# RWKV chunks of a hybrid trunk: one elementwise instruction for both directions or both heads, score products in column halves of the array

## The chip, the cores and the metric

One core of a Trainium2 chip runs the whole program in one launch. The metric is the device time of one execution in microseconds: the kernel before takes 3569.35 us, the median of 3 runs (3568.7 to 3575.61). The engines named here are TensorE (PE in the profile, PEld for its weight loads), VectorE (DVE), ScalarE (ACT), GpSimd (POOL) and SyncE (SP), whose in-order queue issues most DMAs.

## What is computed

A trunk of two layers over 1024 latent and 256 context tokens. Each layer has a token mixer with three groups of heads (RWKV-7 in both directions, windowed attention, neighbourhood attention) and a mixture of experts. The change touches the RWKV group alone: four heads of 64 channels, a state of 64 by 64 per head and direction, fed token by token.

```python
def _rwkv7_step(state, inp):
    r, w, k, v, kk, a = inp
    sk = jnp.einsum('dbhvk,dbhk->dbhv', state, kk)
    state = state * w[..., None, :] - sk[..., :, None] * (kk * a)[..., None, :] + v[..., :, None] * k[..., None, :]
    return state, jnp.einsum('dbhvk,dbhk->dbhv', state, r)
```

Here `d` is the direction (2), `h` the head (4). The 1280 tokens are taken in the order context, latents for the forward direction and with both parts reversed for the backward one; the two outputs of a token are added later.

## The kernel before

The recurrence runs in chunks of 64 tokens. `rwkv()` makes 10 steps per layer; a step handles 128 tokens, that is two chunks (index `c`), of both directions (`d`). Heads lie in pairs: `hp` is the pair (2), and `e` the head in it, whose 64 channels stand in partitions 0 to 63 or 64 to 127 (`hom[e]`, the home half). So a step has 16 units of (d, hp, c, e), in 8 columns of two halves.

`front(st)` prepares a step, one step ahead of its use: `ld` and `lwa` are loaded, the matmuls of L733 give decay and gate inputs, four scans (L744) accumulate the log decay, and the products `L1` (kk and r times decays, L774 and L775: head 0 on VectorE, head 1 on GpSimd), `bk` (L782 on VectorE, L783 on GpSimd) and `bw` (L786) follow.

The step itself then does this, all in fp32:

- L807: 16 transposes turn `bw` into two PSUM tiles `pb`, one for each head, which ScalarE copies to `L2` (L810).
- L822: 16 matmuls `pa`, with 64 rows and all 128 columns of the array, multiply the pair (b, k) of a unit with its pair (kk, r). One matmul so gives four 64 by 64 blocks. VectorE takes them out under masks: `L1`'s other half (L827), `Ly` (L829), and `low` of the backward direction (L831).
- L838: 8 matmuls `pf` give the forward direction's `low`, masked by L839.
- `inv16()` inverts the 16 by 16 diagonal blocks of `low`: `low` goes to DRAM (`lan`) and comes back with another layout (`al`), VectorE does some 30 small instructions (L948 to L955), and the result goes by DRAM (`inv`) into `z16` and `zt16`.
- `mm8` (L851) is called three times with 16 matmuls each, `pe`, `pzt` and `pz`, 64 columns wide, and VectorE combines them (L855 to L857): this joins the blocks of 16 to blocks of 32. L862 to L876 join those to 64.
- Two substeps `s` then advance the state `X`: `px` (L902), a copy `xy` on ScalarE, `pu` (L910), its negation into `X` (L911, L912), `pmy` (L924, L922), the next state (L928), and the output `ys`, four adds of 64 by 128 (L933). `xw` (L895) is the decayed state on GpSimd; `new_pvu` (L711) copies the values into the next `X` with four ScalarE instructions.
- At the step's end two DMAs store `ys` (L938); `values()` loads the next values with two DMAs.

Beside this chain TensorE has independent work: the projections for the two attentions (`in_BC`: L526 to L528 and L537 to L539, products of fp16 high and low parts) are generated piecewise by `more()` between the parts of a step. Every engine runs its own list in order. The lists are written at build time by a scheduler, which mixes the chain of one step, the preparation of the next and the projections.

## Time and profile before

| | before |
|---|---|
| median of 3 runs | 3569.35 us (3568.7 to 3575.61) |
| the profiled execution's own time | 3569.75 us |
| its span in the profile | 3568.1 us |
| TensorE busy over the span | 2943.9 us |
| VectorE busy over the span | 2283.7 us |
| ScalarE busy over the span | 1544.1 us |
| GpSimd busy over the span | 996.8 us |
| mean granted TensorE clock | 0.889 |

The span runs from the first to the last instruction of one execution; 1.65 us of the execution's time lie around it. The RWKV recurrence with the projections beside it takes the stretch from 225 to 734 us in the first layer and from 2004 to 2490 us in the second. Elsewhere (the input projection, attention, output projection, experts) nothing is changed. Busy time of TensorE counts a matmul from its start to its modelled end, so that many overlap; how fast a group of equal matmuls really goes is read from the distance of the starts of groups that follow each other. An fp32 matmul is two records in the trace (a transpose one), so that x32 stands for 16 matmuls. Tiles `L1`, `z16_0` and the like are named `L`, `z` in the rows, and the three uses of `mm8` all stand at L851.

### The profile page before, as it was taken

The page shows a single profiled execution, that of the slowest core. Times are in us where ns is not written, and L with a number is a line of the kernel's source. Part 1 is how long each engine was busy: PE and PEld are TensorE (multiplying, and loading weights), DVE is VectorE, ACT ScalarE, POOL GpSimd, SP SyncE. Part 2 cuts the span into 40 slices and gives each one's busy share as a digit, 9 for nine tenths or more (in the row PEclk, how much of TensorE's full clock was granted, in tenths as well). Part 3 has the DMA queues.
Part 4 walks back from the last instruction along what each step waited for, and adds up shares of the span by engine and source line. Part 5 has one row for each costly group of instructions (what it writes and reads, how often), then busy time and mean ns, then how long its engine had stood idle before and what let it go on. Part 6 is the DMA issues. An engine that isn't in the chain of part 4 may idle for free. (4 is left out here: it accounts for less than half of the span.)

```text
span 3568.1 us, 71262 instructions
## 1 busy us (share of the span) xinstructions
PE 2943.9 (83%) x28620; PEld 1838.5 (52%) x28620; DVE 2283.7 (64%) x4614; ACT 1544.1 (43%) x2769; POOL 996.8 (28%) x998
## 2 busy tenths in 40 slices
PE   7998888989997888888737988898889867777875
PEld 4656556666754434444326555666666443334432
DVE  4257777467768474547688677783776845555765
ACT  4334344346633153546544434343465314434641
POOL 2022443134424111110065225331433321101103
PEclk9989899989998889899868988899899978889977
DMA  9864343372455889999862432443732769999976
GB/s 372 282 206 110 79 108 87 92 212 78 114 202 170 291 327 353 365 378 355 343 228 80 156 100 71 105 104 87 204 107 72 257 238 352 379 389 379 340 265 226
DMA packets 469245, 773.13 MB, mean 217 GB/s; under 512 B 211920, under 2 KB 341616, under 8 KB 452272
## 3 DMA queue, kind: packets, MB, share of 16 engines
q1 hardware_dynamic: 431824, 697.84, 56.9%
q0 software_dynamic: 36368, 68.07, 5.7%
q8 instruction: 228, 3.74, 0.4%
q10 hardware_dynamic: 720, 2.62, 0.3%
q14 instruction: 105, 0.86, 0.1%
HBM read 653.31 MB, written 114.97 MB: 215 GB/s over the span
## 5 line engine op out<-in xcount | busy, mean ns | idle before, releaser
L1662 PE MATMUL pgate<-wgp,hT 128*64 128x512 f16 (+2 forms) x1704 | 371.7, 388 | 130.8 <-ACT wgp L1611 76.6
L1662 PEld LDWEIGHTS <-hT 128*64 128x64 f16 (+2 forms) x3408 | 210.9, 110 | 365.9 <-issue 195.5
L526 PE MATMUL acc<-hH,wH 128*128 128x256 f16 (+2 forms) x1040 | 344.8, 335 | 15.2 <-DVE hH L483 13.0
L527 PE MATMUL acc<-hL,wH 128*128 128x256 f16 (+2 forms) x1040 | 345.3, 333 | 9.5 <-POOL hL L484 9.4
L528 PE MATMUL acc<-hH,wL 128*128 128x256 f16 (+2 forms) x1040 | 345.3, 333 | 0.0
L1662 PE MATMUL pgate<-wup,hT 128*32 128x256 f16 (+1 forms) x1224 | 212.8, 362 | 24.5 <-DVE wup L1612 13.7
L1193 POOL TENSOR_SCALAR s<-s,rd 128x640 f32<-128x640 f32 (+2 forms) x216 | 172.8, 800 | 211.5 <-DVE rd L1189 96.4
L1702 PE MATMUL pd<-wdp,gT 128*64 128x512 f16 (+2 forms) x1704 | 213.1, 358 | 21.7 <-DVE gT L1689 14.9
L1612 DVE SCALAR_TENSOR_TENSOR wgp<-wg,wgp 128x2048 f16<-128x2048 f32 x74 | 166.6, 2286 | 93.4 <-ACT wgp L1611 93.4
L1620 POOL DMA_INDIRECT xg<-hmoe,map x69 | 78.3, 1136 | 527.7 <-PE ptx L1626 491.8
L1612 DVE SCALAR_TENSOR_TENSOR wdp<-wd,wdp 128x2048 f16<-128x2048 f32 x74 | 166.6, 2288 | 71.8 <-ACT wdp L1611 71.8
L1182 ACT ACTIVATE s<-s,nm 128x640 f32<-128x640 f32 (+2 forms) x216 | 164.5, 763 | 68.2 <-DVE nm L1179 50.4
L1206 PE MATMUL po<-pt,vt 128*64 128x128 f32 x1920 | 170.5, 291 | 19.6 <-DVE pt L1197 15.0
L1612 DVE SCALAR_TENSOR_TENSOR wup<-wu,wup 128x2048 f16<-128x2048 f32 x74 | 166.2, 2287 | 31.1 <-ACT wup L1611 31.0
L1291 PE MATMUL acco<-wo,o 128*128 128x512 f16 x756 | 175.9, 386 | 0.0
L1611 ACT ACTIVATE wgp<-wg 128x2048 f16<-128x2048 f32 x74 | 137.6, 1903 | 74.1 <-DMA wg<-w_gate 56.7
L1611 ACT ACTIVATE wdp<-wd 128x2048 f16<-128x2048 f32 x74 | 137.2, 1902 | 73.7 <-DMA wd<-w_down 69.3
L1702 PEld LDWEIGHTS <-gT 128*64 128x64 f16 (+2 forms) x1704 | 95.1, 105 | 124.9 <-DVE gT L1689 20.7
L1715 POOL DMA_DIRECT2D ys<-y x66 | 51.8, 784 | 384.4 <-DVE y L1709 215.5
L1611 ACT ACTIVATE wup<-wu 128x2048 f16<-128x2048 f32 x74 | 137.3, 1904 | 44.4 <-DMA wu<-w_up 41.7
L1163 PE MATMUL pss<-k,qs 128*128 128x256 f16 (+1 forms) x552 | 129.3, 272 | 31.8 <-DVE mx L1176 18.3
L1670 ACT ACTIVATE sg<-pgate 64x256 f32<-64x256 f32 (+2 forms) x86 | 42.7, 496 | 246.9 <-PE pgate L1662 246.8
(420 smaller groups left out, 7429.1 us busy)
## 6 DMA issues: line engine op xcount, KB each, us to landing
wu<-w_up SPq DMA_DIRECT2D x64, 2048.0 KB
wd<-w_down SPq DMA_DIRECT2D x64, 2048.0 KB
wg<-w_gate SPq DMA_DIRECT2D x64, 2048.0 KB
wmod<-w_mod SPq DMA_DIRECT2D x96, 512.0 KB
w<-w_in SPq DMA_DIRECT2D x41, 512.0 KB
ld<-ys SPq DMA_DIRECT2D x40, 384.0 KB
z<-inv SPq DMA_DIRECT2D x80, 128.0 KB
ys<-y POOLq DMA_DIRECT2D x20, 512.0 KB, 10.5
```

Source lines behind the costliest of these rows:

```text
L526: self.nc.tensor.matmul(ov, H[:, k, :], hh, start=k == 0, stop=False)
L527: self.nc.tensor.matmul(ov, H[:, k, :], hl, start=False, stop=False)
L528: self.nc.tensor.matmul(ov, Lo[:, k, :], hh, start=False, stop=k == KD - 1)
L1163: te.matmul(pss[:, o:o + n], qs[:, e, Q], k1[:, e, k0:k0 + n], start=True, stop=False)
L1182: a.activation(s2[:, e, :nk], s2[:, e, :nk], AF.Exp, bias=nm[:, e:e + 1], scale=1.0 / SS, accum_out=den[:, e:e + 1])
L1193: g.tensor_scalar(s2[:, e, :nk], s2[:, e, :nk], rd[:, e:e + 1], SC_Q, OP.mult, OP.mult)
L1206: te.matmul(po[64 * e:64 * e + 64, 0:P], vt[:, kb, 64 * e:64 * e + 64], pt[:, e, x * P:x * P + P], start=x == 0, stop=x == len(kbs) - 1)
L1291: te.matmul(acc, o[:, zo, k] if k < KD - 1 else self.og_last[:, zo, tok], wo[:, zw, k, c], start=k == 0 and y == 0, stop=k == KD - 1 and y ...
L1611: nc.scalar.mul(t[:, 0, c], w[:, c], SC_W)
L1612: nc.vector.scalar_tensor_tensor(t[:, 1, c], w[:, c], SC_W, t[:, 0, c], OP.mult, OP.subtract)
L1662: te.matmul(p[off + i * m:off + i * m + m, :n], part(hT, zh)[:, k, o:o + m], part(w, zw)[:, k, i * n:i * n + n], start=k == 0 and y == 0, ...
L1702: te.matmul(t, part(gT, zh)[:, k, :m], part(wd, zw)[:, k, i * n:i * n + n], start=k == 0 and y == 0, stop=k == 3 and y == len(parts) - 1)
```

## The change

The layout of the tiles is turned so that equal operations of both directions, or of both heads of a pair, are one instruction, and the score products are regrouped by what is taken from them:

- `bw`'s transposes: for head 0 as before; for head 1 each one becomes two ordinary fp32 matmuls with the identity, which put the two 64 by 64 blocks into the halves that the later steps want.
- `pa` gives way to `pk` (k against kk and r, 128 columns, written to the other half of the partitions: 64 rows and 64 columns of the array, both heads in one PSUM tile), `pr` (b against r) and `pf` (b against kk), 16 matmuls each.
- The masks: `L1` as before (4 instructions of 64 by 512), `Ly` one of 128 by 512 for four of 64 by 256, `low` one of 128 by 512 for three.
- `L1`'s products are all on VectorE, 4 of 64 by 512 instead of 4 of 64 by 256 there and 4 on GpSimd. `bk`: one of 128 by 512 on each of VectorE and GpSimd, for two of 64 by 512. The scans: two of 256 for four of 128.
- `mm8` computes and combines only the halves of the columns that can change: 32 columns for 64, and VectorE's three instructions have 256 elements for 512.
- `ys`: one add of 128 by 256 per substep for four of 64 by 128, stored at once by two DMAs per substep (four per step for two). The values come by three DMAs per step for two, and `new_pvu` makes two copies of 64 by 512 for four of 64 by 256. `L2`'s copies are two of 128 by 512 for four of 128 by 256.

```diff
+        E4 = rp.tile([P, 8, 64], F32, name=f"E4{l}")
+        g.memset(E4, 0.0)
...
         vt = {}
         def values(st):
             vt[st] = rp.tile([P, 2, 2, 2, 64], F32, tag="vt", name="vt", bufs=2)
-            for d, seg in enumerate((FSEG[st], BSEG[st])):
-                nc.sync.dma_start(vt[st][:, d], self.vst[:, 2 * seg:2 * seg + 2])
+            nc.sync.dma_start(vt[st][:, :, 0], self.vst[:, 2 * FSEG[st]:2 * FSEG[st] + 2])
+            for s in range(2):
+                nc.sync.dma_start(vt[st][:, s, 1], self.vst[:, 2 * BSEG[st] + 1 - s])
         def new_pvu(st, s):
             t = rp.tile([P, 2, 2, 2, 2, 64], F32, tag="pvu", name="pvu", bufs=2)
-            for d in range(2):
-                for e in range(2):
-                    o = hom[1 - e]
-                    a.copy(t[o, d, :, :, e, :], vt[st][o, d, s if d == 0 else 1 - s].unsqueeze(1).to_broadcast([64, 2, 2, 64]))
+            for e in range(2):
+                o = hom[1 - e]
+                a.copy(t[o, :, :, :, e, :].rearrange("p x d h v -> p x (d h) v"),
+                       vt[st][o, s].rearrange("p d h v -> p (d h) v").unsqueeze(1).to_broadcast([64, 2, 4, 64]))
             return t
...
             for d in range(2):
-                for hp in range(2):
-                    v.tensor_tensor_scan(cum[:, d, hp], k2("scan"), th[:, d, hp], 0.0, OP.mult, OP.add)
+                v.tensor_tensor_scan(cum[:, d].rearrange("p h t -> p (h t)"), k2("scan"), th[:, d].rearrange("p h t -> p (h t)"), 0.0, OP.mult, OP.add)
...
-            L1v = L1.rearrange("p d c h e s t -> p d h e s c t")
-            bku = bk.rearrange("p d h c s t -> p (d h c) s t")
-            for d in range(2):
-                for e in range(2):
-                    eng = v if e == 0 else g
-                    eng.tensor_tensor(L1v[hom[e], d, :, e, e], chv(kk_)[hom[e], d], chv(ex)[hom[e], d], OP.mult)
-                    eng.tensor_tensor(L1v[hom[e], d, :, e, 1 - e], chv(r_)[hom[e], d], chv(cum)[hom[e], d], OP.mult)
+            def pieces(x):
+                return x.rearrange("p d h (c t) -> p d h c t", t=64).rearrange("p d h c t -> p d (h c) t")
             def units(x):
                 return x.rearrange("p d h (c t) -> p (d h c) t", t=64)
+            bku = bk.rearrange("p d h c s t -> p (d h c) s t")
+            v.scalar_tensor_tensor(bku[:, :, 0], units(b2), 0.5, units(wv), OP.mult, OP.mult)
+            g.tensor_tensor(bku[:, :, 1], units(kd), units(wv), OP.mult)
+            L1p = L1.rearrange("p d h c e s t -> p d (h c) e s t")
             for e in range(2):
                 o = hom[e]
-                v.scalar_tensor_tensor(bku[o, :, e], units(b2)[o], 0.5, units(wv)[o], OP.mult, OP.mult)
-                g.tensor_tensor(bku[o, :, 1 - e], units(kd)[o], units(wv)[o], OP.mult)
+                for i, (x, y) in enumerate(((kk_, ex), (r_, cum))):
+                    v.tensor_tensor(L1p[o, :, :, e, i], pieces(x)[o], pieces(y)[o], OP.mult)
...
-                        for e in range(2):
-                            te.transpose(pbs[e][:, i * 64:i * 64 + 64], bw[hom[e], d, hp, c].rearrange("p s t -> p (s t)"), self.ident[hom[e], hom[e]])
+                        o = slice(i * 64, i * 64 + 64)
+                        te.transpose(pbs[0][:, o], bw[hom[0], d, hp, c].rearrange("p s t -> p (s t)"), self.ident[hom[0], hom[0]])
+                        for z in range(2):
+                            te.matmul(pbs[1][hom[1 - z], o], bw[hom[1], d, hp, c, z, :], self.ident[hom[1], hom[1]], start=True, stop=True)
             for e, pb in enumerate(pbs):
-                for d in range(2):
-                    a.copy(L2[:, d, :, :, e].rearrange("p c h t -> p h c t"), pb[:, 256 * d:256 * d + 256].rearrange("p (h c t) -> p h c t", h=2, c=2))
...
+                a.copy(L2[:, :, :, :, e].rearrange("p d h c t -> p (d h c) t"), pb.rearrange("p (u t) -> p u t", t=64))
...
             for d in range(2):
-                pas = [ps.tile([P, 512], F32, tag=tag, name="pa") for _ in range(2)]
+                pk = ps.tile([P, 4, 128], F32, tag=tag, name="pk")
                 for hp in range(2):
                     for c in range(2):
-                        i = 2 * hp + c
                         for e in range(2):
-                            te.matmul(pas[e][:, i * 128:i * 128 + 128], bk[hom[e], d, hp, c].rearrange("p s t -> p (s t)"),
-                                      L1[hom[e], d, c, hp, e].rearrange("p s t -> p (s t)"), start=True, stop=True)
-                for e, pa in enumerate(pas):
-                    home, oth = hom[e], hom[1 - e]
-                    pav = pa.rearrange("p (h c s t) -> p h c s t", h=2, c=2, s=2)
-                    v.tensor_tensor(L1[oth, d, :, :, e].rearrange("p c h s t -> p h c (s t)"), pav[oth].rearrange("p h c s t -> p h c (s t)"),
-                                    mask(f"mL1_{d}", oth, 128), OP.mult)
-                    v.tensor_tensor(Ly[home, d].rearrange("p c h t -> p h c t"), pav[home, :, :, 1 - e], mask(f"mR_{d}", home, 64), OP.mult)
-                    if d == 1:
-                        v.tensor_tensor(low[home, 1], pav[home, :, :, e], mask("mLow", home, 64), OP.mult)
-            pf = ps.tile([P, 512], F32, tag=tag, name="pf")
-            for hp in range(2):
-                for c in range(2):
-                    for e in range(2):
-                        i = 2 * hp + c
-                        te.matmul(pf[hom[e], i * 64:i * 64 + 64], L1[hom[e], 0, c, hp, e, e, :], bk[hom[e], 0, hp, c, e, :], start=True, stop=True)
-            v.tensor_tensor(low[:, 0], pf[:, 0:256].rearrange("p (h c t) -> p h c t", h=2, c=2), mask("mLow", slice(0, 128), 64), OP.mult)
+                            te.matmul(pk[hom[1 - e], 2 * hp + c], bk[hom[e], d, hp, c, 1, :],
+                                      L1[hom[e], d, hp, c, e].rearrange("p s t -> p (s t)"), start=True, stop=True)
+                for e in range(2):
+                    o = hom[1 - e]
+                    v.tensor_tensor(L1[o, d, :, :, e].rearrange("p h c s t -> p (h c) (s t)"), pk[o],
+                                    k2(f"mL1_{d}")[o].unsqueeze(1).to_broadcast([64, 4, 128]), OP.mult)
+            pr = ps.tile([P, 8, 64], F32, tag=tag, name="pr")
+            pf = ps.tile([P, 8, 64], F32, tag=tag, name="pf")
+            for d in range(2):
+                for hp in range(2):
+                    for c in range(2):
+                        for e in range(2):
+                            i = 4 * d + 2 * hp + c
+                            b_, K_, r1 = bk[hom[e], d, hp, c, 0, :], L1[hom[e], d, hp, c, e, 0, :], L1[hom[e], d, hp, c, e, 1, :]
+                            te.matmul(pr[hom[e], i], b_, r1, start=True, stop=True)
+                            x, y = (K_, b_) if d == 0 else (b_, K_)
+                            te.matmul(pf[hom[e], i], x, y, start=True, stop=True)
+            v.tensor_tensor(Ly.rearrange("p d h c t -> p d (h c) t"), pr.rearrange("p (d u) t -> p d u t", d=2),
+                            k2("mR").rearrange("p (d t) -> p d t", d=2).unsqueeze(2).to_broadcast([P, 2, 4, 64]), OP.mult)
+            v.tensor_tensor(low.rearrange("p d h c t -> p (d h c) t"), pf, k2("mLow").unsqueeze(1).to_broadcast([P, 8, 64]), OP.mult)
...
             def mm8(name, lt, rh):
-                o = psi.tile([P, 512], F32, tag="i", name=name)
+                o = psi.tile([P, 8, 2, 16], F32, tag="i", name=name)
                 for u in range(8):
                     for e in range(2):
-                        te.matmul(o[hom[e], u * 64:u * 64 + 64], lt[hom[e], u, :], rh[hom[e], u, :], start=True, stop=True)
-                return o.rearrange("p (u t) -> p u t", t=64)
-            E = rp.tile([P, 8, 64], F32, tag="E", name="E", bufs=1)
-            v.tensor_tensor(E, mm8("pe4", lowu, zt16), k2("mE4").unsqueeze(1).to_broadcast([P, 8, 64]), OP.mult)
-            v.tensor_tensor(zt16, zt16, mm8("pzt", z16, E), OP.subtract)
-            v.tensor_tensor(z16, z16, mm8("pz", E, z16), OP.subtract)
+                        te.matmul(o[hom[e], u], lt[hom[e], u, :], rh[hom[e], u], start=True, stop=True)
+                return o
+            lo16, up16 = halves(z16)[:, :, :, 0], halves(zt16)[:, :, :, 1]
+            Eh = halves(E4)[:, :, :, 1]
+            v.tensor_tensor(Eh, mm8("pe4", lowu, up16), k2("mE4").rearrange("p (g t) -> p g t", t=16).unsqueeze(1).to_broadcast([P, 8, 2, 16]), OP.mult)
+            pzt = mm8("pzt", z16, Eh)
+            v.tensor_tensor(up16, up16, pzt, OP.subtract)
+            v.tensor_tensor(lo16, lo16, mm8("pz", E4, lo16), OP.subtract)
...
-            ys = rp.tile([P, 2, 2, 2, 64], F32, tag="ys", name="ys")
...
+                cs = (s, 1 - s)
...
-                for d in range(2):
-                    c = s if d == 0 else 1 - s
-                    for hp in range(2):
-                        for e in range(2):
-                            for sl in range(2):
-                                te.matmul(px[hom[sl], d, hp, e, :], L1[:, d, c, hp, e, sl, :], X[:, d, 0, hp, e, :], start=True, stop=True)
+                for sl in range(2):
+                    for d in range(2):
+                        for hp in range(2):
+                            for e in range(2):
+                                te.matmul(px[hom[e ^ sl], sl, d, hp, :], L1[:, d, hp, cs[d], e, sl, :], X[:, 0, d, hp, e, :], start=True, stop=True)
...
-                for e in range(2):
-                    o = hom[1 - e]
-                    for d in range(2):
-                        c = s if d == 0 else 1 - s
-                        v.tensor_tensor(ys[o, d, c], pm[o, 1, d], xy[o, d, :, e, :], OP.add)
+                        v.tensor_tensor(nx[hom[e], 0, :, :, e, :], pm[hom[e], 0], xw[hom[e]], OP.add)
+                ys = rp.tile([P, 2, 2, 64], F32, tag="ys", name="ys", bufs=2)
+                v.tensor_tensor(ys, pm[:, 1], xy[:, 1], OP.add)
+                for d in range(2):
+                    nc.sync.dma_start(y_d[d, 2 * seg[d] + cs[d]], ys[:, d])
...
-            for d in range(2):
-                nc.sync.dma_start(y_d[d, 2 * seg[d]:2 * seg[d] + 2].rearrange("c p h t -> p c h t"), ys[:, d])
```

The scheduler writes new lists for all engines. Three places, all in the first layer's step 4 (counted from 0), show what the prediction speaks of.

TensorE, the transposition of `bw`; `pu` belongs to the state's chain of an earlier step, `prope` and `acc` are projections. Before:

```order
L528 MATMUL acc<-hH_223,wL 128x512
L807 MATMUL pb<-c_58,bw 128x64 x3
L910 MATMUL pu_4020<-xy,z_1_3895 64x64 x4
L910 MATMUL pu_4020<-xy,z_0_3891 64x64 x4
L807 MATMUL pb<-c_58,bw 128x64 x13
L1066 MATMUL prope<-qf,c_58 128x512
```

and in the change:

```order
L812 MATMUL pb<-c_58,bw 64x64 x2
L932 MATMUL pmy<-pvu,L_3756 64x64
L810 MATMUL pb<-c_58,bw 128x64
L932 MATMUL pmy<-pvu,L_3756 64x64 x7
L930 MATMUL pmy<-pvu,Ly 64x64 x8
L812 MATMUL pb<-c_58,bw 64x64 x2
L810 MATMUL pb<-c_58,bw 128x64
```

Sixteen transposes in two runs became eight single transposes, each followed by two 64 by 64 matmuls, with the state's `pmy` among them.

TensorE, the score products (`px` and `pe` belong to the chains of earlier steps). Before, with eight more `pa` somewhat earlier:

```order
L902 MATMUL px<-pvu,L_3062 64x64 x16
L851 MATMUL pe_4409<-z_1_4405,low 64x64
L822 MATMUL pa<-L_4215,bk 128x128 x3
L851 MATMUL pe_4409<-z_1_4405,low 64x64 x15
L822 MATMUL pa<-L_4215,bk 128x128 x5
L528 LDWEIGHTS wL
```

and in the change:

```order
L822 MATMUL pk<-L_4233,bk 64x128 x6
L859 MATMUL pe_4444<-z_1_4441,low 64x32
L822 MATMUL pk<-L_4233,bk 64x128 x7
L859 MATMUL pe_4444<-z_1_4441,low 64x32 x15
L822 MATMUL pk<-L_4233,bk 64x128 x3
```

The `pa` of the two heads stand in separate runs, since each head has its own PSUM tile; the 16 `pk` of both heads stand closer, head after head. A piece of projection later the change has this, where before 8 `pf` stood:

```order
L836 MATMUL pr<-L_4233,bk 64x64 x6
L859 MATMUL pzt<-E_1987,z_0_4437 64x32 x16
L839 MATMUL pf<-bk,L_4233 64x64 x6
L836 MATMUL pr<-L_4233,bk 64x64
L839 MATMUL pf<-bk,L_4233 64x64
```

There are 32 of these in all, and from the last rows on `pr` and `pf` take turns.

VectorE, the masks of the score products and the work of the next step between them. Before:

```order
L855 TENSOR_TENSOR E<-pe_4409,c_1967 128x512
L775 TENSOR_TENSOR L_4725<-ld,cum 64x2x2x64 x2
L827 TENSOR_TENSOR L_4215<-pa,c_1967 64x2x2x128
L829 TENSOR_TENSOR Ly<-pa,c_1967 64x2x2x64
L831 TENSOR_TENSOR low<-pa,c_1967 64x256
```

and in the change:

```order
L826 TENSOR_TENSOR L_4233<-pk,c_1967 64x4x128 x2
L864 TENSOR_TENSOR E_1987<-pe_4444,c_1967 128x16x16
L826 TENSOR_TENSOR L_4233<-pk,c_1967 64x4x128 x2
L504 SCALAR_TENSOR_TENSOR wL<-w,wH 128x1024
L866 TENSOR_TENSOR z_1_4441<-z_1_4441,pzt 128x16x16
L867 TENSOR_TENSOR z_0_4437<-z_0_4437,pz 128x16x16
L840 TENSOR_TENSOR Ly<-pr,c_1967 128x512
L842 TENSOR_TENSOR low<-pf,c_1967 128x512
```

Before, the last three rows come once more for the other head, and two pairs of L827 and L829 stand earlier. In the change `Ly` and `low` are one row each, after the combination to blocks of 32 of the step before.

## Rows read from the trace of the kernel before

**Rows 1.** The page's first part: busy us, share and instructions of each engine

```profile
PE 2943.9 (83%) x28620; PEld 1838.5 (52%) x28620; DVE 2283.7 (64%) x4614; ACT 1544.1 (43%) x2769; POOL 996.8 (28%) x998
```

**Rows 2.** Windows of the mixing stretches: length, PE, PEld, DVE, ACT, POOL busy, PEclk

```profile
225.00:734.00 509.00, 447.83 (x6042) 321.00 (x6039) 336.26 (x779) 199.66 (x496) 179.05 (x177) 0.91 0.40 107
2004.00:2490.00 486.00, 432.47 (x5742) 305.93 (x5738) 333.82 (x759) 190.21 (x477) 176.43 (x163) 0.89 0.36 96
```

**Rows 3.** TensorE's waits, first layer (two), then second; total us, times, longest

```profile
PE pe L851 <- DMA z<-inv: 27.2, 12, 4.2
...
PE pmy L924 <- DVE pvu L912: 6.1, 5, 2.7
...
PE pmy L924 <- DVE pvu L912: 19.3, 5, 9.2
```

**Rows 4.** Windows of L822, L851, L807, L838 alone, in that order: sum rows

```profile
sum 995.00, PE 82.27 PEld 67.84; mean PE 41.13 PEld 33.92
...
sum 995.00, PE 86.23 PEld 73.14; mean PE 43.12 PEld 36.57
...
sum 995.00, PE 19.35 PEld 14.76; mean PE 9.67 PEld 7.38
...
sum 995.00, PE 15.13 PEld 12.07; mean PE 7.56 PEld 6.04
```

**Rows 5.** TensorE's timeline: start us, us, line, names, shapes, count

```profile
306.74 1.15 PE L851 MATMUL pzt<-E,z 64*64 64x64 f32 x32
307.82 1.16 PE L822 MATMUL pa<-L,bk 64*128 64x128 f32 x16
308.91 0.23 PE L538 MATMUL accn<-wH,hL 128*128 128x128 f16 x1
```

**Rows 6.** The same view, a few us later

```profile
312.68 1.16 PE L822 MATMUL pa<-L,bk 64*128 64x128 f32 x8
313.76 0.69 PE L862 MATMUL pe<-z,low 32*32 32x32 f32 x32
314.38 0.68 PE L838 MATMUL pf<-bk,L 64*64 64x64 f32 x16
```

**Rows 7.** The same view, where two shapes of the array alternate

```profile
299.81 0.33 PE L851 MATMUL pe<-z,low 64*64 64x64 f32 x2 [3.35 <-DMA z<-inv]
300.07 0.34 PE L807 MATMUL pb<-c,bw 64*128 64x64 f32 x4
300.34 0.23 PE L537 MATMUL accn<-wH,hH 128*128 128x128 f16 x1
```

**Rows 8.** VectorE's groups by line, 225 to 690 us (busy us, mean ns)

```profile
L827 DVE TENSOR_TENSOR L<-pa,c 64x512 f32<-64x512 f32 x40 | 27.4, 684 | 16.6 <-PE pa L822 16.3
L775 DVE TENSOR_TENSOR L<-ld,cum 64x256 f32<-64x256 f32 x20 | 24.4, 1257 | 0.1
L782 DVE SCALAR_TENSOR_TENSOR bk<-th,wv 64x512 f32<-64x512 f32 x20 | 21.6, 1080 | 0.6
L774 DVE TENSOR_TENSOR L<-ld,ex 64x256 f32<-64x256 f32 x20 | 19.3, 997 | 0.5 <-ACT ex L755 0.4
L933 DVE TENSOR_TENSOR ys<-pmy,xy 64x128 f32<-64x128 f32 x76 | 18.5, 283 | 0.3
L829 DVE TENSOR_TENSOR Ly<-pa,c 64x256 f32<-64x256 f32 x40 | 16.9, 422 | 0.6
```

**Rows 9.** GpSimd's group of the same kind, same stretch

```profile
L774 POOL TENSOR_TENSOR L<-ld,ex 64x256 f32<-64x256 f32 x20 | 19.1, 974 | 50.9 <-ACT ex L755 47.5 <-DMA z<-inv 3.4
```

**Rows 10.** VectorE's timeline inside one inversion

```profile
333.07 1.82 DVE L782 SCALAR_TENSOR_TENSOR bk<-th,wv 64x512 f32<-64x512 f32 x2
...
337.25 2.92 DVE L775 TENSOR_TENSOR L<-ld,cum 64x256 f32<-64x256 f32 x2
340.10 1.26 DVE L954 TENSOR_TENSOR zl<-zl,il 64x44 f32<-64x44 f32 x1
```

**Rows 11.** Waits of SyncE's DMA queue, first layer

```profile
SPq L938 <- DVE ys L933: 16.1, 3, 12.7
```

More of the change, by code (lines that the diff above doesn't have):

```diff
@@ L190, in _consts @@
     for k in range(2):
-        d[f"mL1_{k}"] = np.concatenate([np.concatenate([im[k], sm[k]], 1), np.concatenate([sm[k], im[k]], 1)], 0)
-        d[f"mR_{k}"] = np.concatenate([im[k], im[k]], 0)
+        d[f"mL1_{k}"] = np.tile(np.concatenate([sm[k], im[k]], 1), (2, 1))
+    d["mR"] = np.tile(np.concatenate(im, 1), (2, 1))
     d["mLow"] = np.concatenate([lo, lo], 0)
@@ L195, in _consts @@
     e4 = ((q[:, None] // 32 == q[None, :] // 32) & (q[:, None] % 32 < 16) & (q[None, :] % 32 >= 16)).astype(np.float32)
-    d["mE4"] = np.concatenate([e4, e4], 0)
-    d["scan"] = np.tile((np.arange(128) % 64 != 0).astype(np.float32), (128, 1))
+    d["mE4"] = np.tile(e4[:, q % 32 >= 16], (2, 1))
+    d["scan"] = np.tile((np.arange(256) % 64 != 0).astype(np.float32), (128, 1))
     d["i16"] = np.tile(np.eye(16).reshape(1, 256), (128, 1))
@@ L882, in rwkv @@
                 for e in range(2):
[L883 removed]
+                    g.memset(X[hom[e], 0, :, :, e, :], 0.0)
             if st < 9:
                 values(st + 1)
[L887 removed]
             for s in range(2):
                 last = st == 9 and s == 1
+                cs = (s, 1 - s)
                 if not last:
@@ L906, in rwkv @@
                 for d in range(2):
-                    c = s if d == 0 else 1 - s
                     for hp in range(2):
                         for e in range(2):
-                            te.matmul(pu2[hom[e], d, hp, :], tt[d][hom[e], hp, c, :], xy[hom[e], d, hp, e, :], start=True, stop=True)
-                a.mul(X[0:64, :, 1, :, 0, :], pu2[0:64], -1.0)
-                v.tensor_scalar_mul(X[64:128, :, 1, :, 1, :], pu2[64:128], -1.0)
+                            te.matmul(pu2[hom[e], d, hp, :], tt[d][hom[e], hp, cs[d], :], xy[hom[e], 0, d, hp, :], start=True, stop=True)
+                a.mul(X[0:64, 1, :, :, 0, :], pu2[0:64], -1.0)
+                v.tensor_scalar_mul(X[64:128, 1, :, :, 1, :], pu2[64:128], -1.0)
                 pm = psc.tile([P, 2, 2, 2, 64], F32, tag=tagc, name="pmy")
@@ L916, in rwkv @@
                     for d in range(2):
-                        c = s if d == 0 else 1 - s
                         for hp in range(2):
                             for e in range(2):
-                                U = X[:, d, 1, hp, e, :]
+                                U = X[:, 1, d, hp, e, :]
                                 if y:
-                                    te.matmul(pm[hom[1 - e], 1, d, hp, :], Ly[hom[e], d, c, hp, :], U[hom[e]], start=True, stop=True)
+                                    te.matmul(pm[hom[1 - e], 1, d, hp, :], Ly[hom[e], d, hp, cs[d], :], U[hom[e]], start=True, stop=True)
                                 else:
-                                    te.matmul(pm[hom[e], 0, d, hp, :], L2[:, d, c, hp, e, :], U, start=True, stop=True)
+                                    te.matmul(pm[hom[e], 0, d, hp, :], L2[:, d, hp, cs[d], e, :], U, start=True, stop=True)
                 if not last:
@@ L927, in rwkv @@
                     for e in range(2):
-                        v.tensor_tensor(nx[hom[e], :, 0, :, e, :], pm[hom[e], 0], xw[hom[e]], OP.add)
-                for e in range(2):
-                    o = hom[1 - e]
-                    for d in range(2):
-                        c = s if d == 0 else 1 - s
-                        v.tensor_tensor(ys[o, d, c], pm[o, 1, d], xy[o, d, :, e, :], OP.add)
+                        v.tensor_tensor(nx[hom[e], 0, :, :, e, :], pm[hom[e], 0], xw[hom[e]], OP.add)
[3 more added lines that the diff above has]
+                    nc.sync.dma_start(y_d[d, 2 * seg[d] + cs[d]], ys[:, d])
                 if not last:
```

7 lines of the change are left out of this document (3 added, 4 removed).

## The prediction

> **What bounds the kernel now.** The page's first part comes first: over the whole span TensorE is the busiest engine, with 83%, and VectorE follows with 64% [rows 1]. Such shares mix stages, so the next view is the windows of the two stretches that the change touches [rows 2]. There the reader should see that TensorE is busy for 447.83 of 509 us and for 432.47 of 486, so it idles for 61.2 + 53.5 = 114.7 us. VectorE is busy for some 334 us in each, about two thirds. Nothing else is near. The reason lies in the order of the lists: TensorE has the projections to fill its gaps, so that what a chain of waits costs appears only where the list has put an instruction too early. TensorE's work therefore sets the length, plus what it idles.
>
> The waits say what it idles for [rows 3]. In the first layer `mm8`'s first use waits 27.2 us, in 12 waits, for the `z` that the inversion sends back by DMA; and the state's `pmy` waits for VectorE's negation (L912) 6.1 us there and 19.3 us in the second layer. So the waits lead to VectorE's queue, directly or through the inversion, which is VectorE's work too. The timeline of VectorE inside one inversion shows why it is late [rows 10]: the next step's products stand between its small instructions, L782's pair takes 1.82 us, L775's 2.92, and one small instruction of 44 elements takes 1.26, while `ys` adds of 128 elements take 0.283 on average [rows 8]. GpSimd does its share of the same products then, at 0.974 us for 256 elements [rows 9], while VectorE's L829 does as many in 0.422. The two engines slow each other down.
>
> So there are two accounts: what TensorE must do, which the change alters in four places, and what it idles, which the change shortens through VectorE.
>
> **TensorE's account**, in busy time of both layers. The lines concerned take 82.3 us (`pa`), 86.2 (`mm8`), 19.4 (`pb`) and 15.1 (`pf`) [rows 4]. Prices at full clock come from the distance of starts; the granted clock is 0.91 and 0.89 [rows 2], so I divide new work by 0.9.
>
> *`pb`.* Eight transposes a step are now each followed by two 64 by 64 matmuls: 160 turns in all. Where the trace changes shape in this way [rows 7], one lone 64\*64 matmul costs 0.26 us up to the next group (299.81 to 300.07), and four 64\*128 transposes 0.27 (300.07 to 300.34). A turn then costs at least 0.26 and a quarter of 0.27, 0.33 us, and at most 0.53; I take the middle, 0.43: 160 x 0.43 / 0.9 = 76 us, which is 57 more than now. No row shows a 64\*128 and a 64\*64 group in different row halves of the array one by one; if such run side by side, nothing is added. Ends: 0 and (0.53) 75. I take 57 because rows 7 are nearest. The Trainium skill, TensorEngine Tiling (Array Packing), Key Properties, says that changing the tiling mode, not just the tile, drains the engine; by that the turns cost the 57 us, without it nothing, and the trace agrees with the rule in rows 7.
>
> *`pk`.* Eight `pa` of both heads taken in turn need 1.09 us (307.82 to 308.91) [rows 5], but four of one head alone need 1.08 (312.68 to 313.76) [rows 6], and the old list often has heads apart. The new list takes heads in turn: 40 groups x 1.09 / 0.9 = 48 us, 34 less. If they went as those alone, 96, 14 more.
>
> *`pr` and `pf`.* 32 matmuls a step instead of 8. Sixteen of this kind take 1.08 us (306.74 to 307.82) [rows 5]: 20 x 2.16 / 0.9 = 48, 33 more. In the new list two on the same half follow each other; if half of the overlap is lost, 72, 57 more. I take 33, since a matmul of the other half can start as soon as the second is under way.
>
> *`mm8`.* As many matmuls with 32 columns. L862's sixteen of 32 columns take 0.62 us (313.76 to 314.38) [rows 6] against 1.08: 86.2 x 0.62 / 1.08 = 49.5, 37 less. Those use 32\*32 tiles, so the other end is no gain.
>
> Sum: 57 - 34 + 33 - 37 = **19 us more**; ends 38 less and 146 more.
>
> **VectorE's account**, for one layer [rows 8], a 512-element instruction priced at L827's 0.684, a 256-element one at L829's 0.422. `L1`'s products: 43.7 us become 40 of 64 by 512, between 27 (L827's price) and 43 (L782's, 1.08); say 35, 9 less. `bk`: 21.6 become 10 instructions, about 9, 13 less. Masks: 40 of `Ly` (16.9) and 30 of `low` at 0.422 (12.7) become 20 at 0.684, 16 less. `mm8`'s three: 30 x 0.262, 8 less. `ys`: 18.5 become 20 at 0.422, 10 less. Altogether 56 of 334. GpSimd loses its `L1` products, 19.1 for L774 [rows 9] and about as much for L775, and one of two `bk`.
>
> Of the idle time: per inversion some 2 to 3 us go (0.9 from `bk`, 0.9 from `L1`, up to 1 for a small instruction no longer slowed), against `z` waits of 27.2 / 12 = 2.3 on average, so I take 25 of them; half of the 25.4 us for `pmy`, 13; and 7 of all others, since late masks give PSUM tiles back late. Idle falls by **45 us**; ends 0 and 90. What is late next is the round trips of the inversion by DMA, which stay.
>
> The clock knows two levels here, 1.2 and 2.4 GHz; 0.91 and 0.89 [rows 2] mean 2 x 0.09 x 509 + 2 x 0.11 x 486 = 199 us at the lower one. Ahead of 299.81 TensorE had waited 3.35 us [rows 7], and such waits become fewer. With 40% less idle I take 30 us less at half speed, worth **15**; ends 0 and 40.
>
> **At nothing.** The scans, the values' copies and `L2`'s copies become fewer on engines that have room (ScalarE is busy 200 of 509 us [rows 2]); if ScalarE were late, fewer copies would be a gain. SyncE's queue gets three more DMAs a step, one for the values and two for `ys`, and waits for `ys` twice a step instead of once. Today L938's waits are 16.1 us in three [rows 11]; behind it stand the `low` stores that start an inversion and the loads of the next step. VectorE makes `ys` ahead of `low` in most steps, so the queue waits for `low` anyway; without that cover the same 16.1 us would come once more per layer, 32 in all.
>
> **Sum:** 19 - 45 - 15 = -41. The profiled execution took 3569.75 us, its span 3568.1 with 1.65 around it; the median of the runs is 0.4 below it. So 3528 us.
>
> **Rivals.**
> *Idle does not fall.* The new list is as tight as the old one, and an earlier VectorE only lets its queue wait elsewhere, for the same TensorE. Then the added matmuls count alone: 3570 + 19 = 3589, with turns of 0.53 us 3607; I put it at 3595. It decides as soon as idle and clock give back less than the 19 us. For it: VectorE idles a third of the stretch already, and the DMA round trips stay. Against it: the longest totals of waits end in VectorE's queue [rows 3].
> *No gap between row halves.* The turns of `pb` cost nothing: 57 less, 3471. Against it rows 7, though none shows this very pair.
> *Narrow columns give nothing.* `mm8` stays at 86 us: 37 more, 3565, which is no change. For it: no row has 32 columns on a 64\*64 tile; against it L862's 0.62. The Trainium skill, TensorEngine Tiling (Array Packing), Instruction Overhead, says that a matmul of one column takes as long as one of 60 and advises against taking a factor from a dimension that is already small; by that the 37 us would not come. The trace speaks against it in rows 6.
>
> **How the numbers follow.** A difference below 0.2%, 7 us, cannot be told from none here. The forecast has 0.46 and its own range is 3495 to 3562; no gap 0.12; narrow columns 0.12; idle stays 0.30. Faster: 0.46 + 0.12 = 0.58, the same 0.12, slower 0.30. From 3470 to 3602 the range leaves out half of the second case below and some 0.1 of the last above; it takes in the ends of the unknown prices only where they come one at a time.
>
> **What would show it.** In the profile after: `pb`'s lines busy for some 76 us in both windows together and a timeline of single transposes about 0.4 us apart; `pk` near 48 and its groups of eight at 1.09; `mm8` near 50; VectorE near 280 us per stretch; TensorE's idle near 70 us, with the waits for `z` mostly gone; the clock above 0.9. The forecast is wrong if idle stays above 100 us, or if TensorE's busy time grows by more than 60.

## The result, and the profile after

The changed kernel takes 3619.89 us (median of 4 executions) against 3569.02 for the kernel before, also of 4: ratio 1.0153, interval 1.0126 to 1.0179. It is slower by 51 us, 92 above the predicted 3528 and outside the range. The profiled execution took 3622.83 us.

First part of its page (as [rows 1]):

```profile
PE 3008.0 (83%) x30060; PEld 1882.2 (52%) x30060; DVE 2185.4 (60%) x4334; ACT 1525.9 (42%) x2649; POOL 909.0 (25%) x900
```

Windows of the two stretches, from the first matmul of L737 to the last projection (as [rows 2]; length, busy us of PE, PEld, DVE, ACT, POOL, then PEclk):

```profile
224.00:769.00 545.00, 490.68 (x6736) 352.44 (x6736) 286.99 (x640) 189.90 (x436) 133.28 (x125) 0.88 0.39 102
2050.00:2536.00 486.00, 444.98 (x6412) 316.74 (x6411) 283.44 (x617) 178.49 (x412) 127.65 (x113) 0.90 0.37 95
```

VectorE did what was forecast: 287 and 283 us, predicted 280. TensorE did not. With bounds chosen in the same way (225 to 732, 2004 to 2488) the kernel before has 991 us, 878.2 busy, 112.8 idle; here it is 1031, 935.7 and 95.3. From the clock's column, twice one minus PEclk times the length, some 198 us before and 228 now were at 1.2 GHz. The column has two digits, so this is good to some 8 us; the trace's own clock records give 192 and 231. So of the 53 us between the two profiled executions, 40 lie in these windows: 57.5 more busy (half of the 30 us at low clock, 15, and 42 of work; by the clock records 19 and 38), 17.5 less idle. The other 13 lie outside; some 8 of them are 36 records of the projections (0.215 us from start to start), nearly all of which the new list puts ahead of the second layer's window.

TensorE's waits, two of the first layer's window, then two of the second (as [rows 3]):

```profile
PE pe L859 <- DMA z<-inv: 18.3, 6, 6.2
PE pmy L932 <- DVE pvu L921: 14.5, 4, 6.4
...
PE pmy L932 <- DVE pvu L921: 12.9, 5, 3.9
PE pe L859 <- DMA z<-inv: 6.1, 5, 3.9
```

The two waits are still there, with 51.8 us against 56 before (52.6 in [rows 3], and 3.4 for `z` in the second layer). Busy time by line, both windows: `pk` L822, `pr` L836, `pf` L839, `mm8` L859, then `pb`'s transposes L810 and matmuls L812 (as [rows 4]):

```profile
sum 1031.00, PE 45.72 PEld 36.93; mean PE 22.86 PEld 18.47
...
sum 1031.00, PE 44.34 PEld 36.45; mean PE 22.17 PEld 18.23
...
sum 1031.00, PE 45.09 PEld 38.47; mean PE 22.55 PEld 19.23
...
sum 1031.00, PE 82.38 PEld 73.44; mean PE 41.19 PEld 36.72
...
sum 1031.00, PE 44.30 PEld 22.23; mean PE 22.15 PEld 11.12
...
sum 1031.00, PE 60.42 PEld 36.65; mean PE 30.21 PEld 18.33
```

`mm8` is the line to see: 82.38 with 32 columns, 86.23 with 64 [rows 4]. Busy times of turns overlap, so that their sums say too much; a share that adds up is the distance from each matmul's start to the next start, less idle, summed over a line's records ("slots" below). Slots of both layers, before and after: `pb` 17 and 80 us; `pa` 78, now `pk` 36; `pf` 13, now `pr` and `pf` 58; `mm8` 78 and 70; `pu` of the preparation 41 and 28.

TensorE's timeline where `pb` stands (start, us, line, shape of the array, records):

```profile
240.12 0.38 PE L526 MATMUL acc<-hH,wH 128*128 128x512 f16 x1
240.43 0.27 PE L810 MATMUL pb<-c,bw 64*128 64x64 f32 x1
240.64 0.33 PE L812 MATMUL pb<-c,bw 64*64 64x64 f32 x4
240.90 0.27 PE L810 MATMUL pb<-c,bw 64*128 64x64 f32 x1
...
243.89 0.33 PE L812 MATMUL pb<-c,bw 64*64 64x64 f32 x4
244.15 0.39 PE L527 MATMUL acc<-hL,wH 128*128 128x512 f16 x1
...
244.81 0.55 PE L527 MATMUL acc<-hL,wH 128*128 128x512 f16 x1
245.15 0.63 PE L528 MATMUL acc<-hH,wL 128*128 128x512 f16 x1
245.58 0.63 PE L526 MATMUL acc<-hH,wH 128*128 128x512 f16 x1
```

A turn takes 0.47 us (240.43 to 240.90), eight take 3.72. And right behind them, without any idle, the projections' matmuls go from 0.215 us apart to 0.43. The windows of the turns and of the stretch behind show why: PE is busy throughout, and the clock falls from 1.00 to 0.50:

```profile
241.40:244.80 3.40, 3.40 (x35) 2.25 (x34) 2.96 (x6) 3.17 (x6) 0.00 (x0) 1.00 0.50 135
244.90:248.30 3.40, 3.40 (x10) 1.19 (x9) 3.40 (x3) 1.81 (x4) 2.39 (x2) 0.50 0.09 30
```

By the trace's clock records the clock falls 30 times in the two windows; ahead of nine falls TensorE had been in these turns and had not idled. The stretches at 1.2 GHz behind these nine last 41 us together, and the time at that clock grew by 39. The kernel before has 25 falls, none of that kind.

### The profile page after: what moved, and what is told of

Read it like the earlier page. It is cut to its first block, busy times and chain, and to the rows that moved or that the text cites. A ratio compares the mean times of both kernels' runs of the same rounds, so it can differ in the third digit from the quotient of the medians.

```text
span 3621.2 us, 73649 instructions
## 1 busy us (share of the span) xinstructions
PE 3008.0 (83%) x30060; PEld 1882.2 (52%) x30060; DVE 2185.4 (60%) x4334; ACT 1525.9 (42%) x2649; POOL 909.0 (25%) x900
## 5 line engine op out<-in xcount | busy, mean ns | idle before, releaser
L528 PEld LDWEIGHTS <-wL 128*128 128x128 f16 (+1 forms) x1040 | 106.3, 102 | 87.2 <-issue 28.8
L526 PEld LDWEIGHTS <-wH 128*128 128x128 f16 (+1 forms) x1040 | 106.8, 103 | 78.4 <-issue 23.8
```

Of the source, the lines that this page charges most:

```text
L526: self.nc.tensor.matmul(ov, H[:, k, :], hh, start=k == 0, stop=False)
L528: self.nc.tensor.matmul(ov, Lo[:, k, :], hh, start=False, stop=k == KD - 1)
```

## The experiments

Each kernel of the table ran beside the kernel before, on the same chip. Busy, idle and low-clock time ("low") are TensorE's in both stretches, in us, worked out from windows as above; VectorE's busy time is for the same windows. They come from one profiled execution each, whose own time lies up to 16 us from the median. The edits are shown abridged.

| kernel | median us | ratio to before, interval | busy | idle | low | VectorE |
|---|---|---|---|---|---|---|
| before | 3561 to 3569 | 1 | 878 | 113 | 198 | 670 |
| changed | 3619.89 | 1.0153 (1.0126 to 1.0179) | 936 | 95 | 228 | 570 |
| blocks | 3551.94 | 0.9965 (0.9948 to 0.9982) | 883 | 95 | 166 | 587 |
| transposes | 3586.15 | 1.0060 (1.0038 to 1.0083) | 873 | 135 | 192 | 593 |
| halves in turn | 3653.91 | 1.0241 (1.0210 to 1.0272) | 961 | 99 | 254 | 572 |
| wide `mm8` | 3597.72 | 1.0079 (1.0048 to 1.0110) | 929 | 88 | 193 | 593 |
| before + turns | 3607.65 | 1.0123 (1.0104 to 1.0143) | 948 | 84 | 216 | 658 |
| old products | 3592.25 | 1.0087 (1.0070 to 1.0104) | 886 | 115 | 231 | 637 |
| one product | 3567.86 | 1.0021 (1.0003 to 1.0039) | 865 | 125 | 178 | 597 |
| exchanged `bk` | 3570.52 | 1.0022 (1.0007 to 1.0037) | 869 | 133 | 200 | 610 |
| blocks, one product | 3567.69 | 1.0014 (0.9994 to 1.0034) | 891 | 105 | 189 | 586 |
| blocks, other order | 3578.34 | 1.0041 (1.0028 to 1.0053) | 896 | 111 | 202 | 583 |
| before, other order | 3565.98 | 1.0006 (0.9990 to 1.0023) | 869 | 117 | 167 | 668 |
| changed, other order | 3609.70 | 1.0131 (1.0106 to 1.0155) | 949 | 82 | 258 | 574 |
| blocks, products twice | 3641.84 | 1.0220 (1.0200 to 1.0240) | 925 | 147 | 290 | 654 |
| blocks, shared | 3599.43 | 1.0109 (1.0086 to 1.0132) | 888 | 120 | 192 | 561 |
| other order, shared | 3608.09 | 1.0121 (1.0098 to 1.0144) | 900 | 120 | 203 | 560 |
| one product, shared | 3572.24 | 1.0030 (1.0013 to 1.0046) | 880 | 114 | 189 | 569 |
| before, all on VectorE | 3585.15 | 1.0056 (1.0036 to 1.0076) | 883 | 116 | 200 | 708 |

### `pb`: in blocks, by transposes, and alone

Blocks: all transposes of a step come first, then all matmuls with the identity.

```diff
-  for d.. hp.. c..: transpose(head 0); for z: matmul(head 1, z)
+  for d.. hp.. c..: transpose(head 0)
+  for d.. hp.. c..: for z: matmul(head 1, z)
```

> The changed kernel with one difference: in pb all 8 transposes of a step come first, then all 16 matmuls with the identity, instead of 8 turns of one transpose and two matmuls. The same instructions, another order. Theory 1 (each change of array shape stops TensorE, and the stretch is bound by TensorE): pb's slots, now 80 us in both layers, fall to some 36 us (8 transposes 0.43 us, 16 matmuls at 0.07 us, one change of shape: 1.6 us a step, 20 steps, clock 0.9), and the time from 3620 to 3575 to 3585. Theory 2 (the new list's idle time and clock, not pb, made it slower): the slots may fall but the time stays within 10 us of 3620. Theory 3 (the number of matmuls, not their turns, makes pb dear): slots and time stay, 80 us and 3620.

3552 us, 68 less than the changed kernel. The same instructions in blocks, in its timeline:

```profile
241.10 0.71 PE L812 MATMUL pb<-c,bw 64*128 64x64 f32 x8
241.74 1.15 PE L815 MATMUL pb<-c,bw 64*64 64x64 f32 x32
242.82 0.39 PE L527 MATMUL acc<-hL,wH 128*128 128x512 f16 x1
```

1.72 us a step for 3.72, so a turn's two changes of shape cost 0.25 us. The slots of `pb` are 40 us, for some 36 expected; and of 23 falls of the clock none follows `pb` without idle. The 62 us less at low clock are worth 31 of the 68. Theory 1 holds; its price was too low, since it had left out the clock.

Transposes for both heads:

```diff
+  g.tensor_tensor(bw[head 0], bk[head 0], wt)
+  for z: g.tensor_tensor(bw[head 1, z], bk[head 1, 1 - z], wt)
+  for e: transpose(pbs[e], bw[head e])
```

> The changed kernel with transposes for both heads in pb, as before; so that the blocks land where the later steps want them, GpSimd writes head 1's half of bw with its two blocks exchanged, in 3 instructions a step instead of 1. Theory 1: pb's slots fall from 80 to 17 to 19 us, the time by some 60 us to 3550 to 3570. Theory 2 (list, idle, clock): not below 3600. If e1 and this one both fall, their difference (about 18 us expected) is the price of 16 matmuls against 8 transposes without any turns.

`pb`'s slots fall to 18 us, yet the time only to 3586: idle is 135 us. Waits that the turns had covered would fit, but "blocks", with 40 us of `pb`, idles only 95; one list cannot tell.

The kernel before with the turns and nothing else:

```diff
-  for e: transpose(pbs[e], bw[head e])
+  transpose(pbs[0], bw[head 0]); for z in (1, 0): matmul(pbs[1][half z], bw[head 1, z], ident)
```

> The kernel before with the change's pb alone: head 1's 8 transposes become 16 matmuls with the identity, in turns with head 0's transposes; nothing else. Theory 1 (the turns cost their stops and pull the clock down behind them): slots of pb from 17 to 75 to 85 us, more time at the lower clock, the time from 3565 to 3620 to 3640. Theory 2 (pr, pf and the new list cost it): at most 20 us more than before.

44 us more (37 to 51 by the interval): the turns alone make most of the slowdown. The slots of `pb` are 79 us, and ten of its 34 falls of the clock come behind turns without idle. No run tells the gaps of the turns from the transposes in them as what the clock answers to. Its windows, and its waits for `z` in the first layer:

```profile
226.00:754.00 528.00, 485.47 (x6245) 341.17 (x6245) 326.87 (x779) 198.95 (x495) 177.52 (x173) 0.90 0.38 100
2019.00:2523.00 504.00, 462.32 (x5947) 322.88 (x5946) 330.81 (x758) 192.29 (x477) 177.07 (x165) 0.89 0.34 89
```

```profile
PE pe L853 <- DMA z<-inv: 10.3, 7, 4.3
```

VectorE is as loaded as before (658 against 670), but idle falls from 113 to 84 and the wait for `z` from 27.2 [rows 3] to 10.3. That fits a TensorE that is slower and so reaches its waits later. The 17.5 us of idle that the change saves need no faster VectorE.

### `mm8`, the halves, and single prices

```diff
-  o = [P, 8, 2, 16]; E4, zt16, z16 changed in the half of the columns that can change
+  o = [P, 8, 64]; all 64 columns
```

> The changed kernel with mm8 and its three combining instructions 64 columns wide again (512 elements for 256 on VectorE). Theory W (the load of 64 columns of weights sets the pace, the moving columns hardly count): mm8's slots go from 70 to 78 us and the time to about 3628, hard to tell from no change. Theory C (moving columns set the pace, as the prediction took it, and something else ate the gain): slots and time go up by 25 to 35 us, to 3645 to 3655.

`mm8`'s slots go from 70 to 76 us: theory W. The time falls by 22 us where theory W had 8 more; a mere change of the list moves it as much (below). Next, heads in turn at every matmul:

```diff
-  matmul(pr, ...); matmul(pf, ...)     # per head
+  all of pf, then all of pr
```

> The changed kernel with pf's 16 matmuls all before pr's 16, so that heads (halves of the array) take turns at every matmul; in the changed kernel two matmuls on one half follow each other. If matmuls on the same half cannot overlap, pr and pf fall from 58 us in slots to some 48 (16 in 1.08 us) and the time by up to 10 us, to 3610; if only the number of matmuls counts, slots stay at 55 to 58 and the time within 7 us of 3620.

The slots of `pr` and `pf` are 52 us for 58, and the time is 34 us more: no theory had that. Busy time is 25 us more: 13 are half of the 26 more at low clock, some 8 are 35 records of the projections that lie inside the windows in this list. The work itself hardly grew. Inside these groups, at full clock, a matmul takes 63.4 ns from start to start, against 67.5 with two on a half: a small gain from turns, far from half of the overlap.

> No part of the model is computed: groups of 32 fp32 matmuls by themselves, three times over, heads (array halves) in turn. 64 rows by 64 columns of weights with 64, 32 and 128 moving columns; 32 columns of weights with 32 and 64 moving; 64 moving with two matmuls after each other on the same half; 16 turns of one transpose (64 by 128) and two 64 by 64 matmuls, the same in two blocks, and turns with a plain 64 by 128 matmul for the transpose. Theory W (the weights' columns set the pace): 64 moving 68 ns a matmul, 32 moving at least 60, 128 moving 110, 32 columns of weights with 32 moving 40 or less. Theory C (moving columns set it): 32 moving costs 35 to 45. Turns: 0.45 us each if the change of shape stops the engine, against 0.2 in blocks; if it does not, both 0.2. Same half twice: 68 ns if nothing is lost, 100 and more if a half cannot overlap itself.

This is a program of its own, run once. At full clock (first of the three rounds):

```profile
7.67 2.00 PE L44 MATMUL n<-w 64*64 64x32 f32 x64
9.51 3.69 PE L49 MATMUL n<-w 64*64 64x128 f32 x64
13.13 1.20 PE L55 MATMUL w32n<-w 64*32 64x32 f32 x64
14.75 1.98 PE L61 MATMUL w32n<-w 64*32 64x64 f32 x64 [0.42 <-DVE w32n L58]
16.66 2.13 PE L66 MATMUL same<-w 64*64 64x64 f32 x64
18.71 1.09 PE L72 MATMUL one<-eye,w 64*128 64x64 f32 x14
```

From start to start, 32 matmuls each: 64 columns of weights with 64 moving 64 ns (L66, two after each other on the same half: nothing is lost), with 32 moving 57.5 (L44), with 128 moving 113 (L49). 32 columns of weights with 64 moving 60 (L61); only 32 and 32 gives 37.5 at most (L55, to its end). So neither side alone sets the pace: one of 64 keeps it near 60. The round's first group, 64 by 64 with heads in turn, took 108 ns in all three rounds; its windows in the second and third show the clock at 0.50, and in the first it ends where the clock records begin, so it gives no price at full clock. The build put most turns into blocks here, a few were left; one takes 0.46 us:

```profile
21.51 0.27 PE L72 MATMUL one<-eye,w 64*128 64x64 f32 x1
21.71 0.27 PE L73 MATMUL two<-eye,w 64*64 64x64 f32 x1
...
21.97 0.27 PE L72 MATMUL one<-eye,w 64*128 64x64 f32 x1
```

### TensorE's part of before on the new layout; fewer products

Old products: transposes, `pa` and `pf` as before, everything else as changed.

```diff
-  pk, pr, pf; Ly and low masked in one instruction each
+  pa[e] = bk.T @ L1 (128 x 128), pf for d = 0; masks by head as before
```

> The changed kernel with TensorE's part of before: transposes for both heads, pa and pf in place of pk, pr and pf (so bk in 4 instructions, masks in 11 a step), but with the new layout, the merged scans, values, ys, the products all on VectorE and the narrow mm8. TensorE's own slots should stand some 20 us below before (pu 13, mm8 7), idle some 20 below. Theory 1: 3525 to 3550. If the merges are worth nothing by themselves: 3560 to 3570. If idle grows as in the kernel with transposes (149 us there against 126 before): 3570 to 3590.

3592, 28 us slower than before and above all three theories, although TensorE's list is no longer and VectorE's is lighter (637 against 670). Its windows show idle as before and more at low clock:

```profile
226.00:746.00 520.00, 460.16 (x6016) 333.59 (x6018) 322.45 (x700) 190.96 (x436) 149.74 (x135) 0.88 0.40 105
2026.00:2507.00 481.00, 425.92 (x5692) 301.75 (x5691) 314.20 (x677) 177.39 (x412) 143.84 (x123) 0.89 0.36 94
```

In this list the merges are worth nothing by themselves, which speaks against the prediction's second account.

One product of 128 columns for `d = 1` (on "transposes"; on "blocks"; and on "transposes" with the exchange made in `bk`):

```diff
+  d == 1: matmul(pq[u], b, (kk, r))   # 128 columns, for pr and pf of 64
```

> The kernel with transposes for both heads (3586), and besides for the backward direction one product b against (kk, r) of 128 columns in place of two of 64 (24 matmuls a step for 32). pr and pf together fall from 59 us in slots to some 47; the time by 10 to 15 us to about 3573, if the list leaves idle and clock as they are; a change of more than 25 us either way would say that the list's order counts for more than the work.

> The kernel with pb in blocks (3552), and besides the backward direction's b against (kk, r) as one product of 128 columns (24 matmuls a step for 32). By work: pr and pf from 60 us in slots to some 50, so 3540 to 3545. By the list (if the list's order and the clock count for more): anywhere from 3530 to 3580.

> The kernel with transposes for both heads and one product of 128 columns for the backward direction (3568, idle 133), with head 1's blocks exchanged already in bk (two instructions each on VectorE and GpSimd for one) so that GpSimd writes bw in one instruction again. If GpSimd's exchange held up the transposes and so TensorE: idle from 133 to about 110 and 3540 to 3550. If not: 3560 to 3575.

3568, 3568 and 3571. The first gains 18 us; the second loses 16 although its slots fall from 60 to 54 us; the third gives no sign that GpSimd's exchange is what idles TensorE (133 us without it, 125 with it). All three differences are of the size of the next section's.

### The same work in another order

```diff
-  for e in range(2):   # pk, pr, pf (pa and pf in the kernel before)
+  for e in (1, 0):
```

> The kernel with pb in blocks (3552), with the two heads in the other order in pk, pr and pf: not one instruction more or less. What it differs by is what the written list alone does, through idle time and clock. If work decides: 3545 to 3560. If the list decides: more than 15 us either way.

> The kernel before with the two heads in the other order in pa and pf; not one instruction more or less. Tells how much of a time is the written list's. If before is an ordinary list: 3545 to 3585. If it is a lucky one, as one that was chosen among many would be: 3580 to 3610.

> The changed kernel, turns and all, with the two heads in the other order in pk, pr and pf; not one instruction more or less. If the slowdown is the turns' and the work's: 3595 to 3645, still above before in either order. If it was this one list's bad luck: 3565 to 3590.

The lists are written anew at each build. The order of the heads moves "blocks" by 26 us, the kernel before by 2, the changed kernel by 10. The slowdown is there in both orders (3620 and 3610 against 3569 and 3566). What differs by less than some 25 us, like "wide `mm8`", the one product of 128 columns or the 12 us that "blocks" is better than before, is not to be put down to the work, and the 28 us of "old products" hardly. "Blocks" is the one kernel faster than both; in the other order of heads it is slower than before.

### Where VectorE's load counts

```diff
-  for e in range(2):          # products of L1
+  for e in (0, 1, 0, 1):
```

> The kernel with pb in blocks (3552), with VectorE's four products of L1 issued twice (the second time with the same result), which puts some 40 us a layer back on VectorE, about what the change took off. Theory V (VectorE's load sets TensorE's idle time, as the prediction took it): idle of both stretches from 109 to about 150, more time at the lower clock, 3590 to 3610. Theory L (each list is written as tight as the engines' expected times allow, so VectorE's load does not show): idle and time within 15 us, 3540 to 3567.

The time is 90 us more, idle 147 and low clock 290. The waits of the first layer (two rows) and of the second (three):

```profile
PE pmy L935 <- DVE pvu L924: 18.0, 11, 4.9
PE pe L862 <- DMA z<-inv: 17.8, 10, 5.3
```

```profile
PE pmy L935 <- DVE pvu L924: 24.5, 10, 4.6
PE pe L862 <- DMA z<-inv: 18.8, 10, 6.0
PE pmy L935 <- ACT pvu L923: 8.8, 3, 4.6
```

Theory V, it seemed. But VectorE's total, 654 us, is not above the 670 of the kernel before, which idles 113. So I moved the same products off VectorE on three lists, and onto it in the kernel before:

```diff
-  v.tensor_tensor(L1p[o, :, :, e, i], ...)
+  (v, g)[e].tensor_tensor(L1p[o, :, :, e, i], ...)
```

> The kernel with pb in blocks (3552), with head 1's two products of L1 a step back on GpSimd, as before the change (64 by 512 each). Theory V (VectorE's load sets TensorE's idle time and clock, and the products that came over from GpSimd ate what the merged instructions freed): VectorE some 20 us a layer less, idle and half the low-clock time together from 183 us to 145 to 165, the time 3515 to 3535. Theory S (the two engines slow each other so much that sharing gains nothing): VectorE falls by under 10 us a layer and the time stays between 3540 and 3565.

> The same edit (head 1's products on GpSimd) on the kernel with the heads in the other order (3578): a second list for the same question, since the two lists differ by 26 us with the same work. Theory V: 3540 to 3560. Theory S: 3563 to 3593.

> The same edit on the kernel with pb in blocks and one product of 128 columns for the backward direction (3568): a third list. Theory V: 3530 to 3550. Theory S: 3553 to 3583.

> The kernel before with all eight products of L1 on VectorE (64 by 256 each), GpSimd without them, nothing else: the one part of the change that puts work on VectorE. Theory V: VectorE some 10 to 20 us a layer more, idle and low clock up, 3580 to 3610. Theory S: VectorE hardly more (its own products get faster without GpSimd beside them), 3550 to 3575.

With VectorE 17 to 26 us lighter the three kernels are 47, 30 and 5 us slower; the last pair's intervals overlap. Theory V falls, and theory S did not expect the loss of the first two either. Putting the products on VectorE in the kernel before costs some 20 us. Over all these kernels VectorE's total (560 to 708 us) tells nothing of idle or clock: the lightest, "other order, shared", idles 120, the heaviest 116. That each list waits for single results at single places, and that the products come too late on either engine when they take longer than the scheduler expected, would fit; no run shows it, and why the doubling costs as much as 90 us stays open.

## Why the prediction was wrong

Against the profiled execution it missed by 94 us: 23 in TensorE's work (42 more in the windows for 19), 27.5 in idle, 30 in the clock, 13 outside (by the clock records 19 in work and 34 in the clock). The turns of `pb`, which the experiments show to cost most, stood in the sum near their price; what failed are the three gains that were to outweigh them: `mm8`, idle and clock. Neither of the prediction's two signs of being wrong came up: idle is 95.3 us where above 100 would have told, and TensorE's busy time grew by 57.5 where over 60 would have. Each sign took one account alone, and both accounts fell short together.

- *`pb`*: right, with the middle of two bounds taken. 0.47 us a turn at full clock against 0.43, 63 us more in slots against 57. The price came from [rows 7], and the rival without a gap between halves is out. The Trainium skill's rule that a change of mode drains the engine (TensorEngine Tiling (Array Packing), Key Properties) agrees with the 0.47 us for a turn against 0.215 in blocks. What the turns do to the clock stood nowhere in the sum.
- *`pk`*: right in kind, 42 us less in slots for 34. *`pr` and `pf`*: 44 more for 33, and the reason weighed there, that half of the overlap on one half is lost, is not it (64 ns with two on a half). `pu` of the preparation, at nothing in the sum, takes 13 less; no run shows why.
- *`mm8`*: the term that was mis-sized, 8 us less for 37. The row taken, L862's [rows 6], has 32 by 32 tiles: there the weights have 32 columns too. The rival "narrow columns" had the mechanism: 57.5 ns against 64. The Trainium skill's advice in TensorEngine Tiling (Array Packing), Instruction Overhead, not to take a tiling factor from a dimension that is already small, agrees with 32 moving columns on 64 of weights (57.5 ns against 64); with 32 on 32 the runs show a gain, 37.5 ns against 57.5.
- *"Idle falls by 45 us"*: the step that failed in kind. It argued from the engine that the waits lead to, to idle time that its lighter load would free. VectorE became lighter as predicted, but each build writes a new list against expected times, and the kernels with the merges and without the turns idle 95 to 135 us against 113. The 17.5 us that went fit a slower TensorE that reaches its waits later: the kernel before with the turns, its VectorE nearly as loaded as before, idles 29 us less.
- *"30 us less at half speed, worth 15"*: the wrong sign. It tied the clock to waits alone. The turns lower it without any wait (nine falls, 41 us); two lists each give 198 and 167 us before, 228 and 258 after.
- The rival "idle does not fall" was put at 3595. With `mm8`'s 37 us it gives 3632: two rivals came together, and the range took them one at a time. That 3632 lies near the measured 3620 is in part luck, since idle did fall by 17.5 us and the clock cost 15 to 19, which that sum leaves out.

## What to carry to other kernels

Keep matmuls of one array shape together: a turn cost 0.25 us more here than the same work in blocks, and the clock behind it. Price a narrower matmul by the wider of its two sides, moving columns and columns of weights, as the sides of 32 and 64 show here. Where lists are written by a scheduler, do not credit a lighter helper engine with TensorE's idle time; measure the same work in two orders first, and believe no difference smaller than theirs.

## What the runs showed of the hardware

- The granted clock fell from 1.00 to 0.50 behind turns of two array shapes in which TensorE never waited: nine of 30 falls in the changed kernel, ten of 34 in the kernel before with the turns, none of 25 and 23 in the kernel before and in "blocks".
- An fp32 matmul on a 64 by 64 tile costs 57.5 ns with 32 moving columns, 64 with 64 and 113 with 128; 32 columns of weights with 64 moving cost 60, with 32 moving 37.5 at most.
- Two matmuls after each other on the same half of the array lose little or nothing: 64 ns in the probe against 67.5 with halves in turn (1.08 us for sixteen [rows 5]), and 67.5 against 63.4 for `pr` and `pf` in the changed kernel and in "halves in turn".
